# A quarter of the gathered experts computed densely in a PEER layer (Trainium2, one core)

## Chip, cores and metric

The kernel runs on one core of a Trainium2 chip, in fp32. The metric is the device time of one execution in microseconds (us); lower is better. PE is the matmul engine, PEld its weight loads, DVE the vector engine, ACT the scalar engine, POOL the GpSimd engine (it issues the gathers), SP the engine that queues plain loads. A round below means four tokens.

## What is computed

Two transformer blocks run over 256 tokens of width 1024; the second ends in a mixture of experts. The change is in the feed-forward part of the first block, a PEER layer: each token picks 8 heads x 16 experts out of 16384 by the best sums of a first and a second key, and sums the chosen experts' outputs.

```python
s = jnp.einsum('thpd,hpnd->thpn', q, sub_keys)          # 128 first keys, 128 second keys
s_top, i_top = lax.top_k(s, K)                          # K = 16
...
cand_idx = i_top[:, :, 0, :, None] * N_KEYS + i_top[:, :, 1, None, :]
best, pos = lax.top_k(cand, K)
idx = jnp.take_along_axis(cand_idx, pos, axis=-1)
g = jax.nn.softmax(best, axis=-1)
u, v = expert_u[idx], expert_v[idx]
act = jax.nn.gelu(jnp.einsum('td,thkd->thk', xt, u))
return jnp.einsum('thk,thkd->td', g * act, v)
```

So an expert is a pair (first key i, second key j) with index 128 i + j, and a row u and a row v of 1024 numbers. On the reference's inputs, counted from these lines, 8531 of the 32768 chosen pairs have j of 96 or more (26.0%); 24237 have a smaller j, 12030 of them for the first 128 tokens and 12207 for the second. Taken by the eight choices that lie side by side on the partitions (half a head), these counts run from 1409 to 1626 of 2048.

## The kernel before

`_front1` computes the first block up to its residual. `_peer_scores` multiplies the modulated h2 (in two float32r parts, high and low, in the tile `hr`) by `w_query` and the keys; `top16` and `route` (on DVE, as lists of steps that `k.fill` puts between other work) find the 16 best, the softmax weights `gT` and the expert indices `idx`, a column of 128 indices for each token. The choices of a token lie on the 128 partitions.

`_peer_experts` loads the first 8 pieces of the second block's `w_ada_2` into four slots of the big SBUF tile `arena` (`_ada_load`), brings h2 into token order (`by_tokens`, tile `ht`), and runs 2 blocks x 32 rounds x 4 tokens. For each token POOL issues one indirect DMA (L840) that fetches 128 rows of u and v (8 KB each, 1.05 MB) into one of ten buffers; PE broadcasts the token's h2 to all partitions by four float32r matmuls into a PSUM tile `bc` (L857: two column halves, high and low part); DVE multiplies it by the u rows and sums (L859). After four tokens ACT applies gelu, DVE multiplies by `gT` into `wz` (L862), and eight fp32 matmuls of 32 columns each add the four tokens' v rows into `acc` (L866). The gather of a buffer waits for the L866 matmuls that read it ten tokens before. At the end of each block `acc` is transposed and added to the residual (L875 to L884).

The instructions' order on each engine is set when the program is built; each engine runs its own list in order and waits for semaphores. SP's list is a queue too: its next load waits until its slot is free. `_front2` and `_moe`, the second block, load 2 MB weight pieces through a ring of slots; `_front2` starts on the slots 3, 4 and 5.

## Time and profile before

| what | value |
|---|---|
| time, median of 3 runs | 1680.46 us (1680.42 to 1681.04) |
| the profiled execution's own time / its span | 1682.16 us / 1680.3 us |
| busy share: PE, DVE, ACT, POOL | 77%, 51%, 18%, 14% |
| mean DMA rate over the span | 354 GB/s |
| moved by the gathers | 268.45 MB of 594.56 MB |

The shares are means over stages with different limits. The gathers run from 349 us to 1013 us, and there the rows of that stretch have to be read.

### The profile page before, as it was taken

Reading aid. Unit: us, or ns where it says so; the run is one execution under the profiler, and the core shown is the slowest. Engines: PE = TensorE matmul, PEld = TensorE weight load, DVE = VectorE, ACT = ScalarE, POOL = GpSimd, SP = SyncE. Lnnn points to the kernel's source line nnn. Section 1 sums busy time; section 2 is a strip of 40 time slices with the busy share of each in tenths; the row PEclk is TensorE's granted clock in tenths of the full one; section 3 lists DMA queues with packets and bytes.
Section 4 is the critical chain, followed back from the end, with each engine's and each line's share of the span. In section 5 each row is a group of like instructions: output and inputs, shape, how many; then the busy total and the mean of one; then the engine's idle time right before and its main releaser. Section 6 shows DMA issues by size and latency. Waiting matters only on the chain.

```text
span 1680.3 us, 19564 instructions
## 1 busy us (share of the span) xinstructions
PE 1301.6 (77%) x7782; PEld 777.2 (46%) x7782; DVE 855.5 (51%) x1844; ACT 308.9 (18%) x545; POOL 242.1 (14%) x260
## 2 busy tenths in 40 slices
PE   5999999957776777777776777999978665665665
PEld 2878898623333333333333335899943221221211
DVE  4779677968884454554555446874442120121111
ACT  3567544210000000100000004443220000000000
POOL 0000000033333343333333320000000000000000
PEclk8999999978889998898889988999989888897888
DMA  9557762699999999999999997564579999999997
GB/s 377 209 224 277 278 249 101 238 371 419 420 421 420 420 420 420 415 420 420 420 420 420 420 410 277 185 250 151 225 312 429 425 427 427 427 426 429 425 429 298
DMA packets 64992, 594.56 MB, mean 354 GB/s; under 512 B 7008, under 2 KB 8064, under 8 KB 12672
## 3 DMA queue, kind: packets, MB, share of 16 engines
q1 hardware_dynamic: 28032, 324.80, 47.5%
q0 software_dynamic: 36864, 268.45, 38.6%
q8 instruction: 63, 1.03, 0.3%
q14 instruction: 33, 0.27, 0.0%
HBM read 592.15 MB, written 1.08 MB: 353 GB/s over the span
## 4 chain that ended last, share of the span: by engine, by line
DMA 43%; PE 37%; DVE 13%; issue 3%; ACT 2%; POOL 1%; SPq 0%; DVEq 0%; POOLq 0%; ACTq 0%
DMA arena<-w 19%; DMA arena<-uv,idx 12%; DMA uv<-uv,idx 9%; PE bc L857 4%; PE ps L274 4%; PE ps L276 4%; PE ps L275 4%; PE acc L866 4%; DVE arena L859 4%; DMA ring<-w 2%; PE ps L1208 2%; DVE uv L859 2%; PE ps L993 2%; PE pa L1141 1%; DVE wl L263 1%
## 5 line engine op out<-in xcount | busy, mean ns | idle before, releaser
L857 PE MATMUL bc<-ht,identr 128*128 128x512 f32 x1024 | 334.8, 455 | 172.9 <-DVE arena L859 114.6
L857 PEld LDWEIGHTS bc<-ht,identr 128*128 128x128 f32 x1024 | 191.1, 207 | 346.5 <-DVE arena L859 168.0
L859 DVE SCALAR_TENSOR_TENSOR arena<-arena,bc 128x1024 f32<-128x1024 f32 x181 | 219.9, 1219 | 170.0 <-PE bc L857 88.4
L840 POOL DMA_INDIRECT arena<-uv,idx x181 | 171.0, 945 | 660.8 <-PE pa L812 348.5
L274 PE MATMUL ps<-hr,wh 128*128 128x256 f32 x648 | 185.7, 287 | 0.0
L275 PE MATMUL ps<-hr,wh 128*128 128x256 f32 x648 | 184.5, 285 | 0.0
L276 PE MATMUL ps<-hr,wl 128*128 128x256 f32 x648 | 184.1, 284 | 0.4 <-DVE wl L263 0.4
L263 DVE TENSOR_TENSOR wl<-arena,wh 128x1024 fp32r<-128x1024 f32 (+1 forms) x116 | 139.6, 1214 | 80.1 <-ACT wh L262 79.6
L1208 PE MATMUL ps<-arena,xg 128*32 128x512 f32 x832 | 116.3, 688 | 56.1 <-DMA arena<-w 56.1
L866 PE MATMUL acc<-arena,wz 128*32 128x512 f32 x724 | 153.5, 736 | 6.5 <-DVE wz L862 6.5
L262 ACT CAST wh<-arena 128x1024 fp32r<-128x1024 f32 (+1 forms) x116 | 119.4, 1041 | 138.6 <-PE ps L275 98.7
L859 DVE SCALAR_TENSOR_TENSOR uv<-uv,bc 128x1024 f32<-128x1024 f32 x75 | 91.2, 1220 | 77.0 <-PE bc L857 45.0
L274 PEld LDWEIGHTS ps<-hr,wh 128*128 128x128 f32 x648 | 124.1, 192 | 5.1 <-issue 2.8
L860 ACT ACTIVATE s<-s 128x4 f32<-128x4 f32 x64 | 13.1, 205 | 615.1 <-DVE arena L859 366.4
L276 PEld LDWEIGHTS ps<-hr,wl 128*128 128x128 f32 x648 | 124.1, 192 | 1.4 <-DVE wl L263 1.1
L275 PEld LDWEIGHTS ps<-hr,wh 128*128 128x128 f32 x648 | 124.1, 192 | 0.9 <-issue 0.8
L1218 DVE TENSOR_TENSOR hid<-hid,ps 128x512 f32<-128x512 f32 x8 | 5.5, 688 | 209.1 <-PE ps L1208 209.1
L1231 PE MATMUL ps<-arena,hidT 128*32 128x512 f32 x400 | 65.5, 765 | 39.0 <-DMA arena<-w 36.0
L866 PE MATMUL acc<-uv,wz 128*32 128x512 f32 x300 | 90.8, 711 | 0.6 <-DVE wz L862 0.5
L1208 PEld LDWEIGHTS ps<-arena,xg 128*32 128x32 f32 x832 | 24.6, 117 | 130.1 <-DMA arena<-w 66.1
L840 POOL DMA_INDIRECT uv<-uv,idx x75 | 70.9, 945 | 87.8 <-PE acc L866 66.7
L866 PEld LDWEIGHTS acc<-arena,wz 128*32 128x32 f32 x724 | 29.1, 127 | 74.7 <-issue 44.8
(360 smaller groups left out, 1535.8 us busy)
## 6 DMA issues: line engine op xcount, KB each, us to landing
arena<-w SPq DMA_DIRECT2D x74, 2048.0 KB, 39.2
arena<-w_ada SPq DMA_DIRECT2D x24, 2048.0 KB, 10.5
arena<-w_in SPq DMA_DIRECT2D x18, 2048.0 KB, 9.0
ring<-w SPq DMA_DIRECT2D x18, 2048.0 KB, 39.2
arena<-w_query SPq DMA_DIRECT2D x4, 2048.0 KB, 11.1
arena<-w SPq DMA_DIRECT2D x6, 1024.0 KB, 15.3
arena<-w_o_lru SPq DMA_DIRECT2D x2, 2048.0 KB, 10.5
arena<-w_out SPq DMA_DIRECT2D x2, 2048.0 KB, 9.4
```

Source lines behind the costliest of these rows:

```text
L262: nc.scalar.copy(hi, w)
L263: nc.vector.tensor_tensor(lo, w, hi.bitcast(F32), ALU.subtract)
L274: nc.tensor.matmul(out, wh[:, c, cs], rh[:, c, :], start=c == 0, stop=False)
L275: nc.tensor.matmul(out, wh[:, c, cs], rl[:, c, :], start=False, stop=False)
L276: nc.tensor.matmul(out, wl[:, c, cs], rh[:, c, :], start=False, stop=c == kc - 1)
L840: nc.gpsimd.indirect_dma_start(out=uv, out_offset=None, in_=ap["uv"], in_offset=bass.IndirectOffsetOnAxis(ap=idx[:, t:t + 1], axis=0))
L857: nc.tensor.matmul(b[:, 512 * h:512 * h + 512], pick, ht[:, tb, a, 512 * h:512 * h + 512], start=a == 0, stop=a == 1)
L859: nc.vector.scalar_tensor_tensor(u, u, 1.0, b, ALU.mult, ALU.mult, accum_out=s4[:, j:j + 1])
L866: nc.tensor.matmul(acc[32 * j:32 * j + 32, 512 * h:512 * h + 512], w[:, j, 31 - r:63 - r], vs[j][:, 512 * h:512 * h + 512], start=r == 0, ...
L993: nc.tensor.matmul(b[:, j * T:(j + 1) * T], w[:, c, (2 * q + j) * P:(2 * q + j + 1) * P], src[:, c, :], start=c == 0, stop=c == 3)
L1208: nc.tensor.matmul(b[32 * j:32 * j + 32, :], xg[:, c, 32 * j:32 * j + 32], w[:, cc, j, :], start=c == 0, stop=c == NC - 1)
L1231: nc.tensor.matmul(y[h][32 * j:32 * j + 32, :], hidT[:, f, 32 * j:32 * j + 32], w[:, j], start=f == 0, stop=f == 3)
```

## The change

The experts are laid out by second key. Those with j below 96 stay in a table of rows `uv`; those of the last 32 second keys (`ND`, `J0`) become two sets of 32 plain matrices, `ud` (u, transposed) and `vd` (v), of 0.5 MB each.

The gather keeps its shape, but an index beyond the table is skipped (`bounds_check`): that row of the buffer keeps what it held, and its weight is set to zero in `gS`. Since skipped rows must hold finite numbers, POOL writes zeros into buffers that held none before (`more`, `last`).

For the 32 dense keys, `activations` multiplies each `ud` matrix (128 first keys) by h2 of all 256 tokens in fp32 (2 x 8 matmuls per call, 16 calls, two of them ahead of the rounds) and applies gelu into `X`. `weigh` builds, for four tokens at a time, the matrix of weights by first and second key: a one-hot comparison of the first keys on POOL (128x128), one of the dense second keys times `gT` on DVE (128x32), an fp32 matmul of the two; DVE multiplies `X` by it. `values` multiplies `X` by each `vd` matrix, four fp32 matmuls of 512 columns, into the two blocks' sums. Rounds 0 to 13 of the first block carry the other 14 calls of `activations`, rounds 14 to 29 four calls of `weigh` each, rounds 1 to 28 of the second block the 32 calls of `values`.

The high and low parts of 64 tokens are stacked on the 128 partitions, so that one matmul with a column of `pair` (a one in both halves) broadcasts their sum: two matmuls for a token where there were four. In the second block the `bc` tiles are halves of 512 columns, since a second sum `acc1` takes PSUM space. The first block's `finish` comes at round 29 of the second. `X` takes the slots 2 and 3, so `w_ada_2` is loaded through two slots instead of four, and `w_ada_2`'s second sum is read out before the rounds. DVE's product is written back to `bc` instead of over u.

```diff
+ND = 32
+J0 = P - ND
...
-    a["uv"] = np.concatenate([f["expert_u"][0], f["expert_v"][0]], axis=1)
+    u, v = (f[n][0].reshape(P, P, D).transpose(1, 0, 2) for n in ("expert_u", "expert_v"))
+    a["uv"] = np.concatenate([u[:J0], v[:J0]], axis=2).reshape(J0 * P, 2 * D)
+    a["ud"] = u[J0:].transpose(0, 2, 1).reshape(ND, NC, P, P).transpose(0, 2, 1, 3).reshape(ND, P, D)
+    a["vd"] = v[J0:]
...
-    hh, hl = k.hr[:, :8, :], k.hr[:, 8:, :]
+    k.hq = k.hr.rearrange("p j t -> p (j t)").rearrange("p (c n m) -> p c n m", c=NC, n=4)
+    hh, hl = (k.hq[:, :, :, 64 * a:64 * a + 64] for a in range(2))
     off[0] = 4 * T
-    _modulate(nc, k, k.col("norm2_g"), k.mod, 3, 4, scratch([NC, T]), k.arena[:, 64 * T:68 * T], hi=hh, lo=hl)
...
-        nc.vector.tensor_copy(identr, k.ident)
+        pair = one.tile([P, 64], F32R, name="pair")
+        nc.vector.tensor_tensor(pair, k.ident[:, :64], k.ident[:, 64:], ALU.add)
...
-        gT = one.tile([P, T], F32, name="gT")
+        iT, jT, gT, gS = (one.tile([P, T], F32, name=n) for n in ("iT", "jT", "gT", "gS"))
...
+        X = k.arena[:, 8 * D:16 * D].rearrange("p (j t) -> p j t", t=T)
+        hT = two.tile([P, NC, T], F32, name="hT", bufs=1)
+        ex = hT.rearrange("p c (n t) -> p c n t", n=4)
+        nc.gpsimd.tensor_tensor(ex, k.hq[:, :, :, :64].bitcast(F32), k.hq[:, :, :, 64:].bitcast(F32), ALU.add)
...
-            yield nc.vector.scalar_tensor_tensor(sel[0], sel[0], 128.0, sel[1], ALU.mult, ALU.add), 0.15
-            yield nc.vector.tensor_copy(idx[:, tsl], b[:, :P]), 0.15
+                nc.tensor.transpose(b[:, half * P:(half + 1) * P], sel[half].rearrange("p h n -> p (h n)"), k.ident)
+            nc.scalar.copy(iT[:, tsl], b[:, :P])
+            yield nc.vector.tensor_copy(jT[:, tsl], b[:, P:2 * P]), 0.15
+            yield nc.vector.scalar_tensor_tensor(idx[:, tsl], jT[:, tsl], 128.0, b[:, :P], ALU.mult, ALU.add), 0.15
...
+            nc.tensor.transpose(b[:, 2 * P:3 * P], e.rearrange("p h n -> p (h n)"), k.ident)
+            nc.scalar.copy(gT[:, tsl], b[:, 2 * P:3 * P])
+            yield nc.vector.scalar_tensor_tensor(gS[:, tsl], jT[:, tsl], float(J0), b[:, 2 * P:3 * P], ALU.is_lt, ALU.mult), 0.15
...
-        ht = one.tile([P, 2, 2, D], F32R, name="ht")
+        ht = one.tile([P, 4, D], F32R, name="ht")
...
+        raws = itertools.cycle([_unit(k, 18), _unit(k, 21), two.tile([P, D], F32, name="raw", bufs=1)])
+        def raw(src):
+            w = next(raws)
+            nc.sync.dma_start(w, src)
+            return w
+        def activations(p):
+            b = k.pa.tile([P, 512], F32, name="pa", tag="pa")
+            for j in range(2):
+                u = raw(ap["ud"][2 * p + j])
+                for c in range(NC):
+                    nc.tensor.matmul(b[:, j * T:(j + 1) * T], u[:, c * P:(c + 1) * P], hT[:, c, :], start=c == 0, stop=c == NC - 1)
+                    if c % 4 == 3 and j + c < NC:
+                        yield
+            nc.scalar.activation(X[:, 2 * p:2 * p + 2, :].rearrange("p j t -> p (j t)"), b, AF.Gelu_apprx_tanh)
+            yield
+        def weigh(t0):
+            b = k.pa.tile([P, 512], F32, name="pa", tag="pa")
+            A = two.tile([P, 4, P], F32, name="hotA", tag="hotA")
+            B = two.tile([P, 4, ND], F32, name="hotB", tag="hotB")
+            for n in range(4):
+                t = t0 + n
+                nc.gpsimd.tensor_scalar(A[:, n, :], k.const("iota"), iT[:, t:t + 1], None, ALU.is_equal)
+                nc.vector.tensor_scalar(B[:, n, :], k.const("iota")[:, J0:], jT[:, t:t + 1], gT[:, t:t + 1], ALU.is_equal, ALU.mult)
+                nc.tensor.matmul(b[:, n * ND:(n + 1) * ND], A[:, n, :], B[:, n, :], start=True, stop=True)
+            xv = X[:, :, t0:t0 + 4].rearrange("p j t -> p t j")
+            nc.vector.tensor_tensor(xv, xv, b[:, :4 * ND].rearrange("p (t j) -> p t j", t=4), ALU.mult)
+            yield
+        def values(n, accs):
+            v = raw(ap["vd"][n])
+            for tb in range(2):
+                for h in range(2):
+                    nc.tensor.matmul(accs[tb][:, 512 * h:512 * h + 512], X[:, n, tb * P:(tb + 1) * P], v[:, 512 * h:512 * h + 512],
+                                     start=False, stop=tb == 0 and n == ND - 1)
+                yield
...
-        ring = itertools.cycle((0, 3, 1, 2))
+        ring = itertools.cycle((0, 1))
...
-        sums = [pb.tile([P, D], F32, name="bc", tag="bc")[:, :512] for _ in range(2)]
+        acc = [py.tile([P, D], F32, name="acc0")]
+        sums = [acc[0][:, 512 * n:512 * n + 512] for n in range(2)]
         _ada_load(nc, load, k.csr2, sums[0], 0, range(4), "w_ada_2")
+        for p in range(EARLY):
+            for _ in activations(p):
+                pass
         k.fill(1e9, (0,))
         by_tokens(1)
         _ada_set(nc, k, one, sums[0], 0, k.mod2, "b_ada_2")
         _ada_load(nc, load, k.csr2, sums[1], 1, range(4), "w_ada_2")
+        _ada_set(nc, k, one, sums[1], 1, k.mod2, "b_ada_2")
...
+        more = k.persist.tile([P, 4 * D], F32, name="uvh", tag="hr")
+        nc.gpsimd.memset(more, 0.0)
+        last = _unit(k, 26, 2)
+        bufs = itertools.cycle([_unit(k, n, 2) for n in (22, 24, 30)] + [more[:, :2 * D], more[:, 2 * D:]]
+                               + [_unit(k, n, 2) for n in (0, 2, 4, 6)] + [last])
+        clear = [last]
...
-            n = next(nv)
-            uv = two.tile([P, 2 * D], F32, name="uv", tag="uv", bufs=GU) if n is None else _unit(k, n, 2)
+            uv = next(bufs)
+            if uv is last and clear:
+                nc.gpsimd.memset(clear.pop(), 0.0)
             nc.gpsimd.indirect_dma_start(out=uv, out_offset=None, in_=ap["uv"],
-                                         in_offset=bass.IndirectOffsetOnAxis(ap=idx[:, t:t + 1], axis=0))
+                                         in_offset=bass.IndirectOffsetOnAxis(ap=idx[:, t:t + 1], axis=0),
+                                         bounds_check=J0 * P - 1, oob_is_err=False)
...
+        def block(tb, pb, halves, work):
+            n = 2 if halves else 1
+            for r in range(32):
+                s4 = two.tile([P, n, 4], F32, name="s4", tag="s4", bufs=4)
+                todo = work(r)
+                for j in range(4):
+                    t = tb * P + 32 * j + r
+                    u, v = rows(t)
+                    vs.append(v)
+                    pick = pair[:, t % 64:t % 64 + 1].to_broadcast([P, P])
+                    w = D // n
+                    for q in range(n):
+                        b = pb.tile([P, w], F32, name="bc", tag="bc")
+                        for h in range(0, w, 512):
+                            nc.tensor.matmul(b[:, h:h + 512], pick, ht[:, t // 64, q * w + h:q * w + h + 512], start=True, stop=True)
+                        nc.vector.scalar_tensor_tensor(b, u[:, q * w:(q + 1) * w], 1.0, b, ALU.mult, ALU.mult,
+                                                       accum_out=s4[:, q, j:j + 1])
+                    if j % 2:
+                        for _ in range(2):
+                            next(todo, None)
...
+                    k.fill(4.5, (1,))
+                for _ in todo:
+                    pass
...
+        queue = iter(range(EARLY, ND // 2))
+        groups = iter(range(0, T, 4))
...
+        def work0(r):
+            p = next(queue, None)
+            if p is not None:
+                yield from activations(p)
+                return
+            k.fill(1e9, (1,))
+            for t0 in itertools.islice(groups, -(-(T // 4) // (32 - (ND // 2 - EARLY)))):
+                yield from weigh(t0)
...
+        left = [0]
...
+        def work1(r):
+            if r:
+                while left[0] < min(ND, r * ND // 28):
+                    left[0] += 1
+                    yield from values(left[0] - 1, acc)
+            if r == 29:
+                finish(0)
+        with tc.tile_pool(name="psum_b", bufs=2, space=PSUM) as pb:
+            block(0, pb, False, work0)
+        for t0 in groups:
+            for _ in weigh(t0):
+                pass
+        with tc.tile_pool(name="psum_y1", bufs=1, space=PSUM) as py1, tc.tile_pool(name="psum_b1", bufs=2, space=PSUM) as pb:
+            acc.append(py1.tile([P, D], F32, name="acc1"))
+            block(1, pb, True, work1)
+            finish(1)
...
+EARLY = 2
...
+        k.hr = k.persist.tile([P, 16, T], F32R, name="hr2", tag="hr")
```

How the rows stand on three engines. First PE, in the first block, a few rounds after the start; `bc` is the broadcast, `acc` the sum over v, `pa` in the change the dense activation of `ud` (in `arena` and `raw`) by h2 (`hT`). Before:

```order
L857 MATMUL bc<-ht,identr 128x512 x16
L866 MATMUL acc<-arena,wz_2980 32x512 x8
L857 MATMUL bc<-ht,identr 128x512 x16
L866 MATMUL acc<-arena,wz_2977 32x512 x3
L866 MATMUL acc<-uv,wz_2977 32x512
L866 MATMUL acc<-arena,wz_2977 32x512 x3
L866 MATMUL acc<-uv,wz_2977 32x512
```

and with the change:

```order
L939 MATMUL bc<-ht,pair 128x512 x4
L838 MATMUL pa<-hT,arena 128x256 x8
L939 MATMUL bc<-ht,pair 128x512 x4
L838 MATMUL pa<-hT,arena 128x256 x8
L953 MATMUL acc_3019<-arena,wz_2979 32x512 x8
L939 MATMUL bc<-ht,pair 128x512 x4
L838 MATMUL pa<-hT,arena 128x256 x8
L939 MATMUL bc<-ht,pair 128x512 x4
L838 MATMUL pa<-hT,raw 128x256 x8
```

A round held 16 broadcasts and 8 sums; it now holds 8 broadcasts, 16 dense matmuls and 8 sums. Next POOL, where the gathers begin; `uvh` is the former `hr`, `hotA` the comparison. Before:

```order
L840 DMA arena<-uv,idx 128x2048 x7
L840 DMA uv<-uv,idx 128x2048 x3
L840 DMA arena<-uv,idx 128x2048 x7
L840 DMA uv<-uv,idx 128x2048 x3
L840 DMA arena<-uv,idx 128x2048 x7
```

and with the change, first where the gathers begin and, after the line of dots, from round 14 on:

```order
L773 TENSOR_TENSOR hT<-hr 128x2048
L903 MEMSET arena 128x2048
L851 TENSOR_SCALAR hotA<-consts,iT 128x128 x7
L904 DMA arena<-uv,idx 128x2048 x2
L893 MEMSET uvh 128x4096
L904 DMA arena<-uv,idx 128x2048
...
L904 DMA arena<-uv,idx 128x2048 x2
L851 TENSOR_SCALAR hotA<-consts,iT 128x128 x8
L904 DMA arena<-uv,idx 128x2048 x2
L851 TENSOR_SCALAR hotA<-consts,iT 128x128 x8
```

POOL's list was gathers alone; seven comparisons now stand ahead of the first gather and a clearing of `uvh` ahead of the third, and later each pair of gathers stands behind eight comparisons. Last DVE in the later part of such a round, where there were four L859 and one L862 and nothing between them; L940 is the product with u, `hotB` the weighted second-key comparison, L855 the product on `X`:

```order
L940 SCALAR_TENSOR_TENSOR bc,s_4547<-arena,bc 128x1024
L852 TENSOR_SCALAR hotB<-consts,jT,gT 128x32 x5
L940 SCALAR_TENSOR_TENSOR bc,s_4547<-arena,bc 128x1024
L855 TENSOR_TENSOR arena<-arena,pa 128x4x32
L852 TENSOR_SCALAR hotB<-consts,jT,gT 128x32 x2
L940 SCALAR_TENSOR_TENSOR bc,s_4547<-arena,bc 128x1024
L855 TENSOR_TENSOR arena<-arena,pa 128x4x32
L852 TENSOR_SCALAR hotB<-consts,jT,gT 128x32
L949 TENSOR_TENSOR wz_2978<-s_4547,gS 128x4
```

Over the whole round sixteen small comparisons and four products on `X` now stand between the four products with u.

## Rows read from the trace of the kernel before

**Rows 1.** The page: share of time in 40 slices, and the gathers' queue.

```profile
PE   5999999957776777777776777999978665665665
DVE  4779677968884454554555446874442120121111
DMA  9557762699999999999999997564579999999997
...
q0 software_dynamic: 36864, 268.45, 38.6%
```

**Rows 2.** Busy time by stretch (PE, PEld, DVE, ACT, POOL, granted clock, DMA, GB/s).

```profile
356.00:500.00 144.00, 107.87 (x454) 53.76 (x454) 122.44 (x345) 7.65 (x19) 54.95 (x58) 0.85 1.01 418
500.00:680.00 180.00, 130.57 (x575) 59.02 (x573) 91.04 (x161) 3.69 (x18) 68.63 (x74) 0.91 1.01 420
680.00:990.00 310.00, 230.27 (x996) 105.01 (x996) 157.50 (x286) 10.25 (x35) 113.62 (x122) 0.89 1.01 419
1040.00:1200.00 160.00, 159.87 (x1122) 144.34 (x1120) 97.16 (x149) 66.29 (x111) 0.00 (x0) 1.00 0.53 199
```

**Rows 3.** The chain of waits inside the gathers: start, us, what.

```profile
578.82 16.96 DMA arena<-uv,idx
595.88 1.24 DVE arena L859 x2
```

**Rows 4.** Timeline of PE: first sum, two broadcasts, and the last two rounds' sums.

```profile
367.76 2.95 PE L866 MATMUL acc<-arena,wz 128*32 128x512 f32 x16
...
569.77 1.19 PE L857 MATMUL bc<-ht,identr 128*128 128x512 f32 x4 [1.30 <-DVE arena L859]
572.26 0.73 PE L857 MATMUL bc<-ht,identr 128*128 128x512 f32 x2 [1.30 <-DVE arena L859]
...
572.92 1.92 PE L866 MATMUL acc<-arena,wz 128*32 128x512 f32 x16
...
996.24 0.62 PE L866 MATMUL acc<-uv,wz 128*32 128x512 f32 x2
1014.61 3.64 PE L866 MATMUL acc<-arena,wz 128*32 128x512 f32 x16 [6.47 <-DVE wz L862]
```

**Rows 5.** Two fp32 lines of PE: duration ns min/median/max, first and last start.

```profile
L608 PE MATMUL ps<-arena x64: 377/379/381, 195.4 to 209.0; 128*128 128x256 f32 x64
L738 PE MATMUL ps<-arena x64: 272/275/377, 275.9 to 318.0; 128*128 128x128 f32 x64
```

**Rows 6.** Timeline of PE before the gathers: float32r matmuls, then fp32 passes of 128 columns.

```profile
290.38 0.28 PE L275 MATMUL ps<-hr,wh 128*128 128x256 f32 x1
...
290.50 0.28 PE L276 MATMUL ps<-hr,wl 128*128 128x256 f32 x1
...
291.03 1.16 PE L738 MATMUL ps<-arena 128*128 128x128 f32 x8
```

**Rows 7.** Groups of DVE and POOL: busy us, mean ns, idle before.

```profile
L1134 DVE TENSOR_SCALAR pick<-consts,slq 128x128 f32<-128x128 f32 x16 | 4.4, 282 | 0.2
L884 DVE SCALAR_TENSOR_TENSOR xT<-pa,mod,xT 128x128 f32<-128x128 f32 x16 | 4.3, 344 | 5.1 <-PE pa L880 5.1
L1218 DVE TENSOR_TENSOR hid<-hid,ps 128x512 f32<-128x512 f32 x8 | 5.5, 688 | 209.1 <-PE ps L1208 209.1
L840 POOL DMA_INDIRECT arena<-uv,idx x181 | 171.0, 945 | 660.8 <-PE pa L812 348.5 <-PE acc L866 262.3 <-issue 29.9
```

**Rows 8.** Timeline of DVE: eight 128x40 products, their span.

```profile
1125.29 1.29 DVE L1033 TENSOR_SCALAR arena<-arena,A 128x40 f32<-128x40 f32 x8
```

**Rows 9.** Timeline of POOL and PE where the gathers begin.

```profile
348.94 1.07 POOL L840 DMA_INDIRECT arena<-uv,idx  x1 [348.48 <-PE pa L812]
350.31 0.93 POOL L840 DMA_INDIRECT arena<-uv,idx  x1 [0.30 <-issue]
...
355.97 1.92 PE L207 MATMUL bc<-arena,csr 128*32 128x512 f32 x16
```

**Rows 10.** Issues of loads from 310 to 360 us: KB each, us to landing.

```profile
arena<-w_ada SPq DMA_DIRECT2D x5, 2048.0 KB, 11.1
```

More of the change, by code (lines that the diff above doesn't have):

```diff
@@ L236, in _stats, with _modulate @@
     return y
-def _modulate(nc, k, gain, mod, s_shift, s_scale, sq, tmp, hi, lo, y=None):
+def _modulate(nc, k, gain, mod, s_shift, s_scale, sq, tmp, hi, lo, y=None, n=1):
     A = tmp[:, 3 * T:3 * T + NC]
@@ L741, in _peer_scores @@
             todo[tb].append(top16(tb, p))
-GU = 3
 def _peer_experts(tc, nc, ap, k):
@@ L761, in _peer_experts @@
         idx = one.tile([P, T], U32, name="idx")
-        gT = one.tile([P, T], F32, name="gT")
-        wz = [one.tile([P, 4, 64], F32, name=f"wz{n}") for n in range(4)]
+        iT, jT, gT, gS = (one.tile([P, T], F32, name=n) for n in ("iT", "jT", "gT", "gS"))
+        wz = [(one if n < 2 else two).tile([P, 4, 64], F32, name=f"wz{n}", bufs=1) for n in range(4)]
         for w in wz:
             nc.vector.memset(w, 0.0)
+        X = k.arena[:, 8 * D:16 * D].rearrange("p (j t) -> p j t", t=T)
+        hT = two.tile([P, NC, T], F32, name="hT", bufs=1)
+        ex = hT.rearrange("p c (n t) -> p c n t", n=4)
+        nc.gpsimd.tensor_tensor(ex, k.hq[:, :, :, :64].bitcast(F32), k.hq[:, :, :, 64:].bitcast(F32), ALU.add)
         def route(tb):
@@ L842, in rows @@
             return uv[:, :D], uv[:, D:]
-        for tb in range(2):
-            acc = py.tile([P, D], F32, name="acc", tag="acc")
-            for r in range(32):
-                s4 = two.tile([P, 4], F32, name="s4", tag="s4", bufs=4)
-                vs = []
-                for j in range(4):
-                    t = tb * P + 32 * j + r
-                    u, v = rows(t)
-                    vs.append(v)
-                    b = pb.tile([P, D], F32, name="bc", tag="bc")
-                    pick = identr[:, 32 * j + r:32 * j + r + 1].to_broadcast([P, P])
-                    for h in range(2):
-                        for a in range(2):
-                            nc.tensor.matmul(b[:, 512 * h:512 * h + 512], pick, ht[:, tb, a, 512 * h:512 * h + 512],
-                                             start=a == 0, stop=a == 1)
-                    nc.vector.scalar_tensor_tensor(u, u, 1.0, b, ALU.mult, ALU.mult, accum_out=s4[:, j:j + 1])
-                nc.scalar.activation(s4, s4, AF.Gelu_apprx_tanh)
-                w = wz[r % 4]
-                nc.vector.tensor_tensor(w[:, :, 31], s4, gT[:, tb * P:(tb + 1) * P].rearrange("p (j r) -> p r j", j=4)[:, r],
-                                        ALU.mult)
-                for h in range(2):
-                    for j in range(4):
-                        nc.tensor.matmul(acc[32 * j:32 * j + 32, 512 * h:512 * h + 512], w[:, j, 31 - r:63 - r],
-                                         vs[j][:, 512 * h:512 * h + 512], start=r == 0, stop=r == 31)
-                if tb == 0:
-                    k.fill(4.5, (1,))
-                    if r == 0:
-                        _ada_set(nc, k, one, sums[1], 1, k.mod2, "b_ada_2")
-            if tb == 0:
-                k.fill(1e9, (1,))
-            y = _unit(k, 8)
-            nc.scalar.copy(y, acc)
@@ L876, in _peer_experts, with finish @@
+        def finish(tb):
+            y = _unit(k, 16)
+            nc.scalar.copy(y, acc[tb])
             for g in range(2):
@@ L884, in _peer_experts @@
                     nc.vector.scalar_tensor_tensor(x, b[:, j * P:(j + 1) * P], k.mod[:, 40 + c:41 + c], x, ALU.mult, ALU.add)
+        def block(tb, pb, halves, work):
+            n = 2 if halves else 1
+            for r in range(32):
+                s4 = two.tile([P, n, 4], F32, name="s4", tag="s4", bufs=4)
+                vs = []
+                todo = work(r)
[14 more added lines that the diff above has]
+                            next(todo, None)
+                if halves:
+                    nc.vector.tensor_tensor(s4[:, 0], s4[:, 0], s4[:, 1], ALU.add)
+                nc.scalar.activation(s4[:, 0], s4[:, 0], AF.Gelu_apprx_tanh)
+                w = wz[r % 4]
+                nc.vector.tensor_tensor(w[:, :, 31], s4[:, 0], gS[:, tb * P:(tb + 1) * P].rearrange("p (j r) -> p r j", j=4)[:, r],
+                                        ALU.mult)
+                for h in range(2):
+                    for j in range(4):
+                        nc.tensor.matmul(acc[tb][32 * j:32 * j + 32, 512 * h:512 * h + 512], w[:, j, 31 - r:63 - r],
+                                         vs[j][:, 512 * h:512 * h + 512], start=r == 0, stop=tb == 1 and r == 31)
+                if tb == 0:
+                    k.fill(4.5, (1,))
+                for _ in todo:
+                    pass
```

39 lines of the change are left out of this document (17 added, 22 removed).

## The prediction

> **What bounds the kernel now.** I read the page's shares over time first. Between 349 and 1013 us the DMA line shows 9 in every slice while PE shows 7 and DVE 4 to 8, and the queue that moves most there is the gathers' [rows 1]. The stretches confirm it: from 500 to 990 us the 16 DMA engines are busy all the time at 419 to 420 GB/s, PE 73% to 74%, DVE 51% [rows 2]. The chain of waits says the same in time: a gather of 17 us, one product on DVE, some PE work, the next gather [rows 3]. So a round of four tokens costs what four gathers cost. The first sum starts at 367.8 us and the 63rd at 996.2, 62 rounds apart [rows 4]: 10.14 us a round, in which 4 x 1.049 = 4.194 MB come in, 0.4136 MB/us in practice. The last round takes 18.4 us, because its gathers share the engines with weight loads.
>
> **The rounds, engine by engine.** PE needs little of the 10.14 us. Four broadcast matmuls take 1.19 us and two take 0.73, so one more costs 0.23; a round's eight sums take 1.92 us from first to last [rows 4]. An fp32 matmul is two passes: L608's 64 passes of 256 columns start within 13.6 us, 0.216 us each, 0.432 per matmul [rows 5]. The dense work per call follows by columns: 16 activations 6.9 us; one value matrix, four matmuls of 512 columns at 0.864, 3.46 us. A weighing matmul moves 32 columns but loads 128 columns of fp32 weights; the nearest rows are eight passes of 128 columns in 1.16 us, of which 0.275 is the last one's length [rows 5, 6]: 0.126 a pass, 0.25 per matmul, as the upper end, since fewer columns cannot take longer.
>
> DVE pays 1.24 us per product [rows 3], about 5.1 a round with the rest. In the first 144 us it is busy 122.4 [rows 2], 8.6 per round, so some 3.5 of the second block's search lie in each early round. POOL pays 0.945 per gather and 0.30 between two issues [rows 7, 9], 5.0 a round.
>
> **Rounds 0 to 13 of the first block.** PE: 8 broadcasts 1.84, 8 sums 1.9, 16 dense matmuls 6.9, together 10.6 us. DMA: 12030 kept rows of 8 KB over 32 rounds are 3.08 MB, plus two `ud` matrices, 1.05 MB: 4.13 MB, 9.98 us at the rate of now. DVE keeps 8.6. The halved broadcast saves 1.84 us and the dense work adds 6.9, so PE takes over from the DMA engines, with hardly anything between the two. I take 10.9, some stalls on top of 10.6. From the first sum on, 13 rounds: 13 x (10.9 - 10.14) = +9.9 us. Bounds: 10.1 and 11.8.
>
> **Rounds 14 to 31.** DMA needs 3.08 MB, 7.45 us; PE 1.84 + 1.9 + 16 x 0.25 = 7.7. DVE: 5.1, sixteen 128x32 comparisons (eight similar 128x40 products span 1.29 us, 0.15 each [rows 8]) 2.4, four 128x128 products from PSUM (0.344 alone [rows 7], about 0.25 in a row) 1.0: 8.5. POOL: 5.0 and sixteen 128x128 comparisons. No POOL comparison is in the trace; below it is DVE's own comparison of this shape, 0.282, above it a gather's issue, 0.945 [rows 7]. I take 0.285, because it is the same operation on the same tile: 5.0 + 4.6 = 9.6 us, so POOL sets these rounds, and the gathers behind the comparisons come late, not the bytes. 16 x (9.6 - 10.14) = -8.6. Rounds 30 and 31 have no weighing; 8.0 for 7.45 of bytes: -4.3.
>
> The Trainium skill weighs on this place from two sides. GPSIMD Engine Reference (Engine selection) has one-input elementwise work there at roughly line rate, which agrees with what I take; Trainium Architecture — The Big Picture (The five engines, in one table) has streaming elementwise 2x slower than DVE. By the second, 0.56 us a comparison, the round would be 14.0 us and the total about 1727. No run here shows either.
>
> **The second block.** DMA: 12207 rows are 3.125 MB a round, and 28 rounds carry 32 value matrices, 0.60 MB each: 3.725 MB, 9.0 us. PE: 1.84 + 1.9 + 1.14 x 3.46 = 7.7; DVE: eight half products (0.688 for 512 columns [rows 7]) and their reads, about 6. So bytes set it. But the kept rows lie unevenly: of the sixteen groups of eight adjacent partitions the fullest keeps 1626 of 2048, 79.4%, against 74.0% on the mean; if a fixed DMA engine serves each group, the gather ends with that one, 3.33 + 0.60 MB, 9.5 us. I take 9.3: 28 x (9.3 - 10.14) = -23.5. Rounds 0, 29 and 30 without values at 8.0: -6.4. The last round I leave as it is.
>
> The Trainium skill, DMA: Bandwidth & Descriptors (Specifications), gives eight partitions per engine as the convention; by it the 9.5 would hold and the total be 6 us higher. No view here parts the engines.
>
> **Ends.** At the start, seven comparisons stand ahead of the first gather (2 us) and the clearing of 4096 columns ahead of the third; no POOL row has its price, by L859's 1.24 us for 1024 columns 4.9, down to nothing. Both hide behind the other start: eight pieces of `w_ada_2` through two slots. The fifth piece's matmuls stand on PE behind the first block's routing, done about 354 us, as now; then only is slot 0 free for the seventh, which lands 11.1 us later [rows 10], the eighth 2 us after it, at 367; its matmuls (1.92 [rows 9]) and the 16 dense ones of round 0 (6.9) stand ahead of the first sum: 376 instead of 367.8, +8. Bounds 3 and 12. At the end the second `w_in_2` piece waits for slot 4, where `finish` now keeps its copy; `_front2` has PE busy 159.9 of 160 us at a DMA share of 0.53 [rows 2], so the work on the first piece covers it: +1.
>
> **Costed at nothing:** the split h2 layout in the 384 matmuls of `_peer_scores` (0.12 us apart [rows 6]; a tenth more would be 4.6 us); the product written to PSUM, where DVE has 1.5 us of room even in rounds 14 to 29; POOL's sum into `hT`, which has the whole score stage to hide in; the bounds check itself, up to twice the issue, which is 3.8 us a round, covered outside rounds 14 to 29 where POOL has 4 us free.
>
> **Sum.** +8 +9.9 -8.6 -4.3 -23.5 -6.4 +1 = -23.9 us. The profiled execution took 1682.2, so 1658.3; it lies 1.7 above the median shown, so 1656.5 us. Its own range, from the bounds of the early rounds, POOL and the second block taken together: 1635 to 1678.
>
> **Rivals.** (a) *The DMA engines set every round.* For: they are at 9 tenths now and the bytes fall from 4.194 to 3.1 MB; against: POOL's 9.6 in rounds 14 to 29. If the comparisons overlap the issues and rows spread evenly, 18 rounds at 7.45, 28 at 9.0, 13 at 9.98, 3 at 7.56: -48.4 -31.9 -2.1 -7.7 +9 = -81, 1599 us. Chance 0.16. (b) *POOL ends it on the other side: its comparisons in rounds 14 to 29.* From 0.38 us each the gain is gone (16 more rounds' worth: 5.0 + 16 x 0.38 = 11.1); at 0.56 the time is 1726. For: they share POOL's one list with gathers, each pair of which waits for eight of them, and they in turn for PE. Against: 0.282 on DVE. Chance 0.17, with times from 1681 to 1726. (c) *Skipped rows cost the DMA engines as much as kept ones*, so that only bytes are added: early rounds 5.24 MB, 12.7 us, +33; second block 4.79 MB, 11.6 us, +41; with the ends 1763. Nothing in the trace shows a skipped row. Chance 0.04.
>
> **Chances.** The forecast has 0.63; it ends 24 us under now, and about 0.08 of it falls within 0.2% (3.4 us, what a measurement of this kernel can tell from no change), 0.01 above. Faster 0.54 + 0.16 = 0.70, same 0.08, slower 0.01 + 0.17 + 0.04 = 0.22. The range goes from 1604, near the end of (a), to 1706, half way through (b).
>
> **What the profile after would show.** Gathers' queue near 198.5 MB; first sum near 376; rounds of 10.9 with PE near full and its granted clock at the upper level, then 9.6 with POOL near full, then 9.3 with the DMA line at 9; POOL comparisons near 0.29 us apart. Wrong if DMA stays at 9 tenths in rounds 14 to 29 (a), if those rounds exceed 11 us (b), if the queue still moves 268 MB (c), or if PE waits for DVE in rounds 0 to 13 so that they take 12.

## The result and the profile after

The changed kernel takes 2068.66 us (median of 4, 2066.27 to 2075.87) against 1680.44: ratio 1.2318, interval 1.2285 to 1.235. The forecast was 1656.5, the range 1604 to 1706. The profiled execution took 2066.81 with a span of 2064.9.

In the views below L838 is the dense activations, L853 the weighing, L863 the value matrices, L953 the sums and L212 the work on `w_ada_2`; in the runs these lines lie up to a few further down. Page of the changed kernel, the lines that answer to [rows 1]:

```profile
PE   5999998798877777655556555578999876666665
...
POOL 0000003233477777312221222120000000000000
PEclk8999999799855556877777787789999998888887
DMA  9566525898655546846555555587654899999997
...
q0 software_dynamic: 36864, 198.60, 26.5%
```

The gathers move 198.60 MB, as forecast. But the DMA line, at 9 through all gathers of before, is at 4 to 6 in most of their slices now. The stretches, columns as in [rows 2]:

```profile
394.00:545.00 151.00, 144.35 (x727) 102.71 (x727) 112.55 (x305) 12.87 (x30) 51.59 (x51) 0.97 0.91 343
550.00:830.00 280.00, 215.27 (x911) 131.34 (x914) 168.90 (x461) 3.49 (x17) 214.70 (x313) 0.61 0.53 183
960.00:1200.00 240.00, 137.22 (x430) 55.49 (x428) 77.14 (x234) 2.67 (x13) 51.43 (x52) 0.78 0.54 196
```

The first is rounds 0 to 13, where PE is the bound as forecast. In the second, rounds 14 to 29, PE and POOL are both busy 77% and the granted clock is 0.61. In the third, the second block, neither an engine nor the DMA line is busy even 60%.

The starts of the sums cut the program into five stages (us; the n-th sum is that of round n, counted from 0; the last column runs to the end of the span):

| kernel | first sum at | sums 0 to 13 | 13 to 32 | 32 to 63 | after sum 63 |
|---|---|---|---|---|---|
| before | 367.8 | 134.5 | 195.2 | 317.1 | 665.7 |
| changed | 394.1 | 155.9 | 300.4 | 537.6 | 677.0 |
| difference | +26 | +21 | +105 | +220 | +11 |

Second block, one round of the chain of waits (start, us, what):

```profile
1001.82 1.92 PE acc L953 x16
1003.74 1.06 PE acc L863 x2
1004.80 0.47 PE bc L939 x2
1005.27 0.86 PE acc L863 x2
1006.12 0.03 PE bc L939
1006.15 8.80 DMA raw<-vd
1014.95 0.04 issue
1015.00 2.08 PE acc L863 x2
1017.07 0.43 PE bc L939
1017.50 1.71 PE acc L863 x2
```

The 8.80 us are a value matrix's load, issued as a matmul of L863 ends and waited for by the next L863. Here is why, in PE's order of one round (a listing of the program, no times; `acc0` and `acc1` are the halves for the first and the second block's tokens):

```
2336 L953 MATMUL acc1_5971<-arena_64,wz3_2980 32x512 x8
2337 L863 MATMUL acc1_5971<-arena_64 128x512
2338 L939 MATMUL bc_6838<-ht_2987,pair_2968 128x512
2339 L939 MATMUL bc_6841<-ht_2987,pair_2968 128x512
2340 L863 MATMUL acc1_5971<-arena_64 128x512
...
2343 L863 MATMUL acc0_3019<-arena_64 128x512
2344 L939 MATMUL bc_6861<-ht_2987,pair_2968 128x512
2345 L863 MATMUL acc0_3019<-arena_64 128x512
```

The `acc1` pair in front is not of the matrix of the `acc0` pair behind it: by the program it is matrix 17, and the `acc0` pair is matrix 20, which is loaded into the same buffer. `acc0` is touched by nothing else any more, so the scheduler let these halves run ahead until all three buffers held a matrix whose second half was still to come; `acc1` is written by each round's sums too and keeps their pace. From then on each round finishes an old matrix, which frees its buffer, and needs the new one in the same buffer a few matmuls later.

Rounds 14 to 29, one round of the chain:

```profile
654.27 0.73 PE bc L939
...
655.56 1.49 PE pa L853 x14
...
657.08 0.41 DVE arena L855
...
659.25 1.47 DVE hotB L852 x5
660.71 1.20 DVE bc L940 x2
...
662.05 0.77 PE bc L939
662.82 3.25 PE pa L853 x16
666.07 1.69 PE bc L939 x3
667.76 3.57 PE acc L953 x16
```

Fourteen passes of L853 take 1.49 us here and sixteen 3.25 a few us later; the sums take 3.57 where [rows 4] has 1.92: TensorE runs at 1.2 GHz for most of the round, at a mean clock of 0.60:

```profile
654.00:671.00 17.00, 13.18 (x60) 8.22 (x56) 10.40 (x29) 0.20 (x1) 13.50 (x21) 0.60 0.56 190
```

And the price asked for, from the groups of POOL (ns: min, median, max):

```profile
L851 POOL TENSOR_SCALAR hotA<-consts,iT x256: 590/596/666, 350.3 to 813.9; 128x128 f32<-128x128 f32 x128
```

### The profile page after: what moved, and what is told of

Read it like the earlier page. It is cut to its first block, busy times and chain, and to the rows that moved or that the text cites. A ratio compares the mean times of both kernels' runs of the same rounds, so it can differ in the third digit from the quotient of the medians.

```text
span 2064.9 us, 22413 instructions
## 1 busy us (share of the span) xinstructions
PE 1554.1 (75%) x8552; PEld 944.1 (46%) x8552; DVE 975.2 (47%) x2452; ACT 320.2 (16%) x566; POOL 419.0 (20%) x519
## 3 DMA queue, kind: packets, MB, share of 16 engines
q0 software_dynamic: 36864, 198.60, 26.5%
## 4 chain that ended last, share of the span: by engine, by line
PE 51%; DMA 33%; DVE 11%; issue 2%; ACT 2%; POOL 0%; SPq 0%; DVEq 0%; ACTq 0%; POOLq 0%
DMA arena<-w 16%; PE acc L863 8%; PE acc L953 7%; DMA arena<-vd 7%; PE bc L939 6%; PE pa L838 5%; DMA raw<-vd 4%; PE pa L853 4%; DMA ring<-w 3%; DVE bc L940 3%; PE ps L282 3%; PE ps L280 3%; PE ps L281 3%; DVE hotB L852 2%; DMA arena<-uv,idx 1%
## 5 line engine op out<-in xcount | busy, mean ns | idle before, releaser
L940 DVE SCALAR_TENSOR_TENSOR bc<-arena,bc 128x512 f32<-128x512 f32 (+1 forms) x306 | 262.9, 880 | 306.5 <-PE bc L939 296.2
L939 PE MATMUL bc<-ht,pair 128*128 128x512 f32 x512 | 297.1, 642 | 111.1 <-DVE bc L940 107.2
L904 POOL DMA_INDIRECT arena<-uv,idx x204 | 206.2, 1011 | 448.2 <-PE acc L953 361.9
L939 PEld LDWEIGHTS bc<-ht,pair 128*128 128x128 f32 x512 | 115.0, 237 | 278.9 <-issue 169.9
L863 PE MATMUL acc<-arena 128*128 128x512 f32 x168 | 116.4, 791 | 124.9 <-DMA arena<-vd 124.9
L953 PE MATMUL acc<-arena,wz 128*32 128x512 f32 x816 | 161.1, 758 | 6.0 <-DVE wz L949 5.8
L851 POOL TENSOR_SCALAR hotA<-consts,iT 128x128 f32<-128x128 f32 x256 | 150.3, 599 | 52.0 <-PE pa L853 52.0
L863 PE MATMUL acc<-raw,arena 128*128 128x512 f32 x88 | 62.3, 802 | 69.1 <-DMA raw<-vd 69.1
L863 PEld LDWEIGHTS acc<-arena 128*128 128x128 f32 x168 | 36.8, 240 | 163.7 <-DMA arena<-vd 131.5
L940 DVE SCALAR_TENSOR_TENSOR bc<-uvh,bc 128x512 f32<-128x512 f32 (+1 forms) x78 | 67.2, 881 | 76.1 <-PE bc L939 75.8
L953 PE MATMUL acc<-uvh,wz 128*32 128x512 f32 x208 | 97.5, 762 | 0.8 <-DVE wz L949 0.8
```

Source lines behind the costliest of these rows:

```text
L851: nc.gpsimd.tensor_scalar(A[:, n, :], k.const("iota"), iT[:, t:t + 1], None, ALU.is_equal)
L863: nc.tensor.matmul(accs[tb][:, 512 * h:512 * h + 512], X[:, n, tb * P:(tb + 1) * P], v[:, 512 * h:512 * h + 512], start=False, stop=tb == ...
L904: nc.gpsimd.indirect_dma_start(out=uv, out_offset=None, in_=ap["uv"], in_offset=bass.IndirectOffsetOnAxis(ap=idx[:, t:t + 1], axis=0), bou ...
L939: nc.tensor.matmul(b[:, h:h + 512], pick, ht[:, t // 64, q * w + h:q * w + h + 512], start=True, stop=True)
L940: nc.vector.scalar_tensor_tensor(b, u[:, q * w:(q + 1) * w], 1.0, b, ALU.mult, ALU.mult, accum_out=s4[:, q, j:j + 1])
L953: nc.tensor.matmul(acc[tb][32 * j:32 * j + 32, 512 * h:512 * h + 512], w[:, j, 31 - r:63 - r], vs[j][:, 512 * h:512 * h + 512], start=r == ...
```

## Experiments

Each ran once, e14_all four times; the kernel before took 1678.73 to 1686.66 beside them. Diffs are against the changed kernel or the run named. Stages as in the table above:

| run | us | first sum | 0 to 13 | 13 to 32 | 32 to 63 | after |
|---|---|---|---|---|---|---|
| e1_order | 1852.16 | 394.2 | 155.8 | 298.8 | 327.3 | 674.1 |
| e2_raw4 | 2054.43 | 389.9 | 154.9 | 300.6 | 531.3 | 675.8 |
| e3_dve | 2038.35 | 390.5 | 155.6 | 271.5 | 541.4 | 677.6 |
| e4_const | 2026.8 | 391.9 | 154.9 | 263.2 | 538.2 | 676.7 |
| e5_order_dve | 1818.8 | 389.4 | 155.6 | 271.0 | 326.8 | 674.2 |
| e6_fill | 1814.66 | 389.4 | 155.4 | 264.0 | 327.1 | 677.0 |
| e7_fill_pool | 1867.42 | 392.3 | 155.4 | 316.9 | 327.0 | 673.8 |
| e8_split | 1814.07 | 392.9 | 156.2 | 299.7 | 289.4 | 673.8 |
| e9_act | 1782.05 | 395.6 | 156.6 | 262.5 | 288.9 | 676.7 |
| e10_act_fill | 1742.49 | 388.2 | 155.6 | 228.2 | 292.2 | 676.5 |
| e11_nd16 | 1785.39 | 374.5 | 189.8 | 242.1 | 301.5 | 674.9 |
| e12_ends | 1736.49 | 383.2 | 154.8 | 231.4 | 288.9 | 676.3 |
| e13_spread | 1866.15 | 399.9 | 148.5 | 351.8 | 291.2 | 673.0 |
| e14_all | 1892.48 | 383.3 | 143.6 | 403.5 | 291.7 | 673.6 |
| e15_all_nofill | 1823.83 | 384.7 | 143.6 | 332.0 | 288.5 | 673.4 |

### The second block: e1_order, e2_raw4, e8_split

```diff
-                    nc.tensor.matmul(accs[tb][...], X[:, n, ...], v[...], ...)
+                    tc.keep_in_program_order(
+                        nc.tensor.matmul(accs[tb][...], X[:, n, ...], v[...], ...))
```

> The changed kernel with one edit: the four matmuls of each value matrix keep the program's order on TensorE, so that the second half follows the first at once. Theory A (order: the first halves stand two matrices ahead of the second halves, so that each load goes out only when TensorE is about to wait for it): the rounds of the second block fall from 19.0 us to 9.3 to 10.5; 26 rounds times 8.5 to 9.7 is 220 to 250 us, so 1815 to 1845 us. Theory B (the loads are slow by themselves, since they share the DMA engines with the gathers): the rounds stay above 17 us and the time above 2010.

1852.16: theory A's mechanism, 7 us above its range, since the rounds with values take 10.7 us and not 9.3 to 10.5. Of the 215 us, 210 come out of the second block, 537.6 to 327.3 us, by an edit that only orders matmuls (below: pinned). A load still takes as long when it is no longer waited for (e8_split, with 8.4 us in the changed kernel):

```profile
arena<-vd SPq DMA_DIRECT2D x21, 512.0 KB, 7.8
```

e2_raw4:

```diff
-        raws = itertools.cycle([_unit(k, 18), _unit(k, 21), two.tile([P, D], F32, name="raw", bufs=1)])
+        raws = itertools.cycle([_unit(k, 18), _unit(k, 21), two.tile([P, D], F32, name="raw", bufs=1),
+                                two.tile([P, D], F32, name="raw2", bufs=1)])
```

> The changed kernel with a fourth buffer for the dense matrices and nothing else. Theory A (order): the first halves run ahead by one matrix more and the wait for a load in each round stays; 2055 to 2075 us. Theory C (three buffers are too few, whatever the order): a load has a round more, the rounds of the second block fall to 10 to 14 us, the time to 1830 to 1950.

2054.43, block 531.3: by the program the `acc0` halves now stand four matrices ahead of the `acc1` halves, where they stood three ahead, so the fourth buffer is held as well. Theory C falls.

e8_split, against e1_order, where `values` now also yields behind each matmul:

```diff
-                    if j % 2:
+                    if halves:
+                        next(todo, None)
+                    elif j % 2:
```

> e1_order with the four matmuls of a value matrix spread over the round, one behind each token's broadcasts, in place of four in a row. Theory S (in e1_order the four stand 3.4 us in a row, while VectorE has only two broadcasts to work on and runs dry): rounds of 9.8 fall to the 9.0 that the bytes need, rounds with two matrices stay longer; 20 to 30 us less than e1_order. Theory T (bytes already set them): within 5 us of 1852.

1814.07, 38 us less: theory S, with more than it asked. Its second block by the window:

```profile
850.00:1130.00 280.00, 255.84 (x974) 97.78 (x966) 176.03 (x546) 10.03 (x34) 116.78 (x118) 0.99 0.99 392
```

DMA is at 0.99: now bytes set the block, and the 28 rounds with values take 9.24 us each. The engines move 392 GB/s at that share, where [rows 2] has 419; why is open.

### Rounds 14 to 29: who makes the one-hots

e3_dve (e4_const only takes the first line away, and A is a tile of zeros, so it leaves out the weights of the dense experts):

```diff
-                nc.gpsimd.tensor_scalar(A[:, n, :], k.const("iota"), iT[:, t:t + 1], None, ALU.is_equal)
+            nc.vector.tensor_tensor(A, k.const("iota")[:, None, :].to_broadcast([P, 4, P]),
+                                    iT[:, t0:t0 + 4, None].to_broadcast([P, 4, P]), ALU.is_equal)
```

> The changed kernel with the comparisons with the first keys made on VectorE, one instruction of 512 columns for four tokens, in place of four on GpSimd. Theory P (GpSimd: 16 comparisons of 0.59 us and four gathers, 14.5 us, and its waits for TensorE set rounds 14 to 29): the rounds go from 17.05 us to what VectorE then has, 10.3 + 4 x 0.65 = 13; 16 x 4 = 65 us less, 2002 us, between 1980 and 2020. Theory Q (TensorE at a granted clock of 0.6 sets them, and GpSimd only waits): above 16 us a round, 2050 or more.

> The changed kernel without the comparisons with the first keys: the matmul that weighs reads one constant tile, so the dense experts get no weight and the output is not the reference's. Theory P (GpSimd): VectorE's 10.3 us set rounds 14 to 29, 10.5 to 12 a round, 80 to 105 us less: 1962 to 1987 us. Theory Q (TensorE at the lower clock): 15.5 us or more a round, 2040 or more.

2038.35 and 2026.8: neither theory's number. The scheduler packs the weighing into about 13 and 9 rounds that still take 16 to 21 us, and most of the others take 6 to 9; so the stage is what can be compared. Without any comparison it falls by 37 of the 105 us that it had gained. What is left in e4_const:

```profile
606.00:726.00 120.00, 108.29 (x462) 82.69 (x454) 76.28 (x250) 1.23 (x6) 23.73 (x24) 0.54 0.44 155
```

PE is busy 90% at a clock of 0.54. GpSimd was one part, about a third.

e5_order_dve joins the pin of e1_order and e3_dve:

> The second halves in order (as e1_order) and the comparisons on VectorE (as e3_dve) together, the ground for the next run. If the two act in different rounds they add: 1852 - 28 = 1824 us, between 1815 and 1835. If the lower clock of rounds 14 to 29 had something to do with the second block's waits: away from that sum by more than 15 us.

1818.8: they add (1852.2 - 28.5 = 1823.7).

### Rounds 14 to 29: the clock

The fill, one matmul for each group, ahead of L855's product (e6_fill is e5_order_dve with it, e7_fill_pool is e1_order with it):

```diff
+            nc.tensor.matmul(b[:, 4 * ND:], A[:, 3, :], hT.rearrange("p c t -> p (c t)")[:, :384], start=True, stop=True)
             xv = X[:, :, t0:t0 + 4].rearrange("p j t -> p t j")
```

> e5_order_dve with one matmul more for each group of four tokens, fp32, 384 columns, into a part of the PSUM tile that nobody reads. It is work that is worth nothing, 0.65 us of TensorE a group at 2.4 GHz and 1.3 at 1.2 GHz. Theory Q (rounds 14 to 29 are long because the weighing matmuls, 128 columns of weights for 32 that move, leave TensorE at 1.2 GHz): the granted clock rises above 0.8 there, a group costs 0.75 + 0.65 in place of 1.75 us and broadcasts and sums take half; 60 to 90 us less than e5_order_dve. Theory R (TensorE's work, not its clock, sets them): 40 to 85 us more.

> The same matmul that is worth nothing, one for each group of four tokens, in e1_order, where GpSimd still makes the comparisons. If the lower clock alone sets rounds 14 to 29, they fall as in e6_fill, to 10 to 12 us, 80 to 110 us less than 1852. If GpSimd's list stands next behind it (16 x 0.59 and 4 x 1.3 are 14.6 us), they fall only to 14.6 to 15.5: 25 to 40 us less, 1812 to 1827. Without an effect of the clock: longer than 1890.

1814.66 and 1867.42: 4 less and 15 more, and no theory had either. Over the sums 13 to 32 the clock rose from 0.69 to 0.83 in e6_fill, where VectorE, which also makes the comparisons there, was busy 206 of 264 us; in e7_fill_pool it rose only from 0.61 to 0.70, with GpSimd busy 225 of 317 us. Inconclusive; a second engine may have stood behind the first. So both were relieved: e9_act, against e8_split, makes the one-hots on ScalarE (`nT` is minus the first key), and e10_act_fill adds the fill to it.

```diff
-                nc.gpsimd.tensor_scalar(A[:, n, :], k.const("iota"), iT[:, t:t + 1], None, ALU.is_equal)
+                nc.scalar.activation(A[:, n, :], k.const("iota"), AF.Abs, bias=nT[:, t:t + 1])
+            nc.scalar.activation(A, A, AF.Relu, bias=1.0, scale=-1.0)
```

> e8_split with the one-hots of the first keys made on ScalarE, which has nothing else to do in these rounds: |iota - key| for each token and 1 - that, cut at zero, for four. GpSimd and VectorE have less to do than in any run before. Theory Q (TensorE at 1.2 GHz with the weighing matmuls sets these rounds): as without comparisons (e4_const) a group costs 1.75 us, all that stands between rounds 13 and 32 takes 263 us in place of 300: 1814 - 37 = 1777 us, between 1765 and 1790. Theory U (VectorE's 1.35 us a group and its products set them): 190 us of VectorE's work for these rounds, 1705 to 1735.

> e9_act with one fp32 matmul of 384 columns that is worth nothing for each group of four tokens. With GpSimd and VectorE relieved, the clock alone is left. Theory Q: the granted clock rises above 0.8 and the time falls by 15 to 45 us against e9_act, though TensorE has more work. Theory R (work, not clock): 40 to 85 us more.

1782.05, inside theory Q's bounds; and 1742.49, 40 us less with 64 matmuls more. The two windows, e9_act first:

```profile
580.00:720.00 140.00, 113.20 (x546) 80.74 (x546) 92.54 (x302) 86.63 (x246) 25.23 (x27) 0.66 0.42 152
```

```profile
580.00:700.00 120.00, 110.22 (x656) 71.62 (x659) 95.69 (x303) 88.33 (x242) 29.82 (x31) 1.00 0.57 202
```

The clock goes from 0.66 to 1.00; added work shortens the stage by 34 us. Over the whole stage the clock goes from 0.71 to 0.96, and PE's busy time falls from 206 to 195 us though it has more matmuls: that the clock gives time back is shown. The scheduler also ordered this stage anew around the added matmuls, so how much of the 34 us is the clock alone is not shown.

### The ends, the early rounds, and everything together

e12_ends, against e10_act_fill:

```diff
-        ring = itertools.cycle((0, 1))
+        ring = itertools.cycle((0, 3, 1))
-            y = _unit(k, 16)
+            y = _unit(k, 8)
```

> e10_act_fill with two edits at the ends: three buffers for the eight pieces of w_ada_2 at the start in place of two, and the copy that finish makes put into a unit of X instead of buffer 4, for which the second piece of w_in_2 waits. Theory of the start (the seventh and eighth pieces are late for want of a buffer): the first sum comes at 376 to 380 in place of 388. Rival: the 48 dense matmuls ahead of the first sum set it; it stays behind 385. Theory of the end (buffer 4): from the last sum to the end 666 to 668 us in place of 676.5, before had 665.7. Rival: over 674. Both together 1720 to 1726 us.

1736.49, above the 1720 to 1726: the first sum comes at 383.2, 5 earlier and between the two theories; the end takes 676.3, so buffer 4 is not its reason.

e13_spread, against e8_split, with `tc.keep_in_program_order` around L838 too:

```diff
-                    if halves:
-                        next(todo, None)
-                    elif j % 2:
-                        for _ in range(2):
-                            next(todo, None)
+                    next(todo, None)
```

> e8_split with the dense activation matmuls of rounds 0 to 13 in the program's order, four behind each token's broadcasts, where there were runs of 8 to 23. Theory V (long runs leave VectorE without broadcasts, TensorE then waits in turn and its clock falls): 13 rounds of 10.8 to 11.2 in place of 12.0; 1799 to 1804 us. Theory W (TensorE's work sets them, whatever the order): within 5 us of 1814. Rounds 14 to 29 stay at 17.

1866.15, outside both. Rounds 0 to 13 fall from 156.2 to 148.5 us, between V and W. But one piece per token rules rounds 14 to 29 as well, which I had overlooked: four comparisons, then a gather, then four more, each behind a matmul. They take 20.5 us in place of 17.

e14_all joins e12_ends and e13_spread, pins L853 as well, shortens the fill to 256 columns and makes the second one-hot so (`iota_4`, `jT_4` and `gT_4` stand here for the views over four tokens; e15_all_nofill is without the fill):

```diff
-                nc.vector.tensor_scalar(B[:, n, :], iota[:, J0:], jT[:, t:t + 1], gT[:, t:t + 1], ALU.is_equal, ALU.mult)
+            nc.vector.tensor_tensor(B, iota_4, jT_4, ALU.is_equal)
+            nc.gpsimd.tensor_tensor(B, B, gT_4, ALU.mult)
```

> All of it together: value and activation matmuls in order and spread, four weighing groups in each of rounds 14 to 29, in order; one-hots of the first key on ScalarE, those of the second as one comparison for four tokens on VectorE and one product on GpSimd; a matmul of 256 columns that is worth nothing for each group; both ends as in e12_ends. Rounds 14 to 29: TensorE 3.8 + 4 x 1.2 = 8.6 us at 2.4 GHz, VectorE 8.3, bytes 7.5, so 9 to 9.8. Against e12_ends (1723): 50 less there and 12 less in rounds 0 to 13; 1660 us, between 1645 and 1680, that is at or below the kernel before. If TensorE falls to 1.2 GHz there all the same: 12 us or more a round and above 1700.

> e14_all without the matmul that is worth nothing. Theory Q: without it the granted clock falls to 0.5 to 0.7 in rounds 14 to 29, the rounds go to 11 to 14 us; 30 to 70 us more than e14_all. If four groups a round, evenly spread, keep the clock by themselves: 5 to 15 us less than e14_all.

1892.48 (1885.18 to 1897.68; ratio 1.1236, 1.1191 to 1.128) and 1823.83. Both forecasts fell: of e14_all the case that came is its last one, the lower clock, and e15_all_nofill is 69 us less where theory Q asked for more. Rounds 0 to 13 now take 143.6 / 13 = 11.0 us. But rounds 14 to 29 take 23.9 us each, at a clock of 0.50 in spite of the fill.

```profile
570.00:880.00 310.00, 240.26 (x832) 156.93 (x824) 98.94 (x220) 100.42 (x273) 73.64 (x104) 0.50 0.40 128
```

```profile
PE bc L949 <- DVE bc L950: 69.7, 39, 1.8
```

```profile
631.78 0.29 DVE L856 TENSOR_TENSOR hotB<-consts,jT 128x128 f32<-128x128 f32 x1 [3.00 <-PE pa L861]
```

Above: what PE waits for in this window (us in all, times, longest), and one wait of VectorE. VectorE, ScalarE and GpSimd are each busy less than a third of the time. PE waits 69.7 of the 310 us for VectorE's product with u (L950), and in VectorE's list that product stands behind steps that wait for the weighing matmuls (L861): the two engines wait for each other in turn. The fill is one step more in this chain and costs 69 us. It helped in e10_act_fill, where PE is busy 92%, and not here, where PE is busy 78%; it was also shorter here, and no run parts the two. Nor does one part the pin of L853 from the one piece per token, which cost 52 us in e13_spread.

e11_nd16, a version with ND = 16, the weights written to X first and both kinds of work spread over all 32 rounds, in order:

> A version worked out from the runs: 16 second keys dense in place of 32 (87.3% of the rows gathered), the weights written first, two groups of four tokens in every round of the first block, with one-hots on ScalarE, the activations (one matrix in every second round) multiplied in by GpSimd before the second block uses them, value matmuls in order and spread as in e8_split, the ada loads through four buffers again. Rounds by bytes: 0.873 x 4.19 + 0.27 = 3.93 MB, 9.5 us, in both blocks; TensorE 7.0 us at 2.4 GHz, VectorE 9 us. If that holds: start +10, 62 rounds 0.64 less each, tail +8: about 1660 us. If the weighing matmuls keep TensorE at 1.2 GHz here too: rounds of the first block of 12 us, 1730.

1785.39, above both cases: the first sum comes at 374.5, but rounds 1 to 12 take 13 to 18 us, and after them rounds with a dense matrix take 14 to 18 us and the others 10. Its weighing is pinned as in e14_all; what holds these rounds was not tried. The best stage of each run with ND = 32 put together (383.2 + 143.6 + 228.2 + 288.5 + 673.0) is 1716.5: no version here beats the kernel before.

## Why the prediction was wrong, point by point

**The step that failed and cost the most** is "So bytes set it" in the second block, 9.3 us a round. I worked out loads by rate and PE by counts and left PE's order out, though the listing of the order had it. The 28 rounds with values took 18.3 us each, and in the round shown 8.8 of them are the wait for a load. With the order mended and the matmuls spread (e8_split) the step is right: 9.24 us each where the sum had 9.3. The stage as a whole is 27.7 less, where the sum had -23.5 and, for rounds 29 and 30, -4.3; there is luck in how well that agrees, since round 29, which carries `finish`, takes 14.5 us for 8.0 and the last round 8.1 where 18.4 were left. The Trainium skill, DMA: Bandwidth & Descriptors (Specifications), gives eight partitions per engine as the convention, by which the 9.5 would hold; the 9.24 do not speak for it, though no run here parts the engines.

**Rounds 14 to 29: "16 x 0.25" on PE and "0.285" on POOL.** Both prices were too low. In the 17.0-us round shown PE is busy 13.2 us and POOL 13.5, forecast 7.7 and 9.6, and PE waits for VectorE's products in the rest. A weighing matmul costs 0.21 us at 2.4 GHz (14 passes in 1.49), as bounded, but the rounds made of them run mostly at 1.2 GHz, which doubles the broadcasts and sums as well. I had the clock in the rows and priced every matmul at its upper level. POOL's comparison is 0.596, 2.1 times VectorE's 0.282: by the prediction's own sum it gives 5.0 + 16 x 0.596 = 14.5 us a round, 1735 us. Of the prediction's two pages of the Trainium skill, the 2x of Trainium Architecture — The Big Picture (The five engines, in one table) agrees with the 0.596, and the line rate of GPSIMD Engine Reference (Engine selection) does not. Rival (b) had the right sign and, of the 105 us of this stage, about the 37 that taking GpSimd off it gave back (e9_act against e8_split). The fill gave back another 34 (e10_act_fill). The last 33 were not taken apart; VectorE is busy 80% there.

**Rounds 0 to 13: 10.9 us.** Right mechanism, PE-bound at full clock, and right size where nothing disturbs: the second to fourth gap are 10.8 each. The mean is 12.0, and PE waits for VectorE on the way, which the prediction had named as a sign of being wrong. Rounds 5 to 9 take 34 to 42 dense passes in place of 32 and last 12.1 to 12.9 us, and round 10 then has none left: PE is busy 6.2 of its 11.6 us, waits for VectorE in the rest, and the clock falls:

```profile
499.72:511.35 11.63, 6.21 (x25) 2.22 (x25) 11.13 (x24) 0.20 (x1) 4.56 (x4) 0.72 0.93 339
```

In order the rounds take 11.0 (e15_all_nofill).

**Start: +8, measured +26.** The seventh piece of `w_ada_2` is late as described. What the prediction missed is again PE's order: the sixth piece's matmuls stand behind a broadcast that waits for VectorE, so the eighth piece, which takes the sixth's slot, is issued at 371.4 and waited for until 380.2, where 367 was forecast.

```profile
366.55 1.22 PE L939 MATMUL bc<-ht,pair 128*128 128x512 f32 x2 [10.64 <-DVE bc L940]
367.70 3.64 PE L212 MATMUL acc<-arena,csr 128*32 128x512 f32 x16
...
380.16 3.64 PE L212 MATMUL acc<-arena,csr 128*32 128x512 f32 x16 [4.96 <-DMA arena<-w_ada]
```

The rest is work at a mean clock of 0.69 from there to the first sum, 3.6 us for 1.9 and 8.7 for 6.9. A third buffer brings 5 back, and in e11_nd16, four buffers and no dense work in front, the first sum comes at 374.5.

**End: +1, measured +11.** The first 40 us after the last sum, of before and of the changed kernel:

```profile
1014.00:1054.00 40.00, 36.28 (x178) 25.24 (x179) 26.23 (x49) 23.10 (x34) 0.00 (x0) 0.94 0.80 316
```

```profile
1388.00:1428.00 40.00, 32.60 (x144) 23.06 (x145) 22.98 (x42) 19.38 (x28) 0.00 (x0) 0.86 0.87 347
```

TensorE does less at a lower clock. Why is open.

**The rivals.** (a) needed engines that follow the bytes; DMA at 0.53 excludes it. (b) had a part, as said. (c) asked for 11.6 us in the second block; e8_split has 9.24. Costed at nothing and right: the bounds check, an issue of 1.01 us for 0.945. The case that came, a wait for a load in a block where bytes were to set the time, was among none of them.

## What to carry to other kernels

Where a scheduler sets the order, read the order of each engine for buffers that are released late: halves of one item that depend on different things drift apart until every buffer is held, and then a prefetch is none. Price matmuls at both clock levels where the rows of before show both. And pin what has nothing to wait for on other engines; a step that waits for three of them may turn overlap into a chain when it is pinned, as e14_all suggests.
